# The last pair of a group of eight, its lent buffers, and the output transposes: another order for the same work

## The chip, the cores and the metric

The kernel runs on one core of one Trainium2 chip. The metric is the device time of one execution in microseconds. The kernel before took 1664.11 us as the median of 3 runs (1663.07 to 1665.39).

The engines are named as in the profile: PE is TensorE (matrix products and transposes), DVE is VectorE, ACT is ScalarE, POOL is GpSimd, SP is SyncE. Each works through its own instructions in the order in which the program writes them and waits, where it must, for what another engine has to deliver first.

## The reference

One layer of a diffusion backbone is applied to 640 tokens (128 context and 512 latent) of width 1024: a SwiGLU FFN as a half step, a token mixer (an mLSTM in both directions and a short convolution), a second SwiGLU FFN as a half step, and a final RMSNorm. The change lies in the second FFN and in the final norm:

```
h = modulate(rmsnorm(x, norm_g[2]), sh2, sc2)
a, b = split(h @ ffn2_w1, 2)              # 1024 -> 2 x 2816
x = x + 0.5 * g2 * ((silu(a) * b) @ ffn2_w2)   # 2816 -> 1024
y = rmsnorm(x, final_norm)                # all of it float32
```

## The kernel before

**Data.** Activations are kept transposed: a tile has 128 channels on its partitions and the 640 tokens along its free axis, in two halves of 320. The product of a 128 x 128 piece of a weight with 320 tokens is made from three matmuls (`three`, lines 242 to 247): the weight and the activation are each split into a rounded high part and a rest, and high x high, high x low and low x high are added up. A split (`split`, lines 73 to 79) is a cast on ACT (L75) and a subtraction on DVE (L79).

**Pairs.** `pair_el` takes two column blocks of a weight and both halves of the tokens as a 2 x 2 block product and does it with seven products instead of eight (`pair_steps`, from line 259). Their order is A11, S1, S2, A12, S3, S4, A22. Each takes 12 matmuls, and each uses one combination of the weights (S1 to S4 are sums or differences made on DVE, L218) and one combination of the activations: 11, 21, 22, T1, T2, T3, T4. Four PSUM tiles a, b, e, c gather the results: A11 goes into a; ACT copies a into b (L273), and S2 is added into b; ACT copies b into c (L283), and S3 is added into c; then c plus the result of S1 (called p5) is put into an SBUF tile (L294, or a copy on ACT and an addition on DVE, L291 and L292, where `spare_v` is set), after which A22 is added into c. The four results are given to the caller's function `ev(column block, half, source)`; the two of the second column block come last and are put into the list `late`.

**What sets the order.** There is no planner; the program order is written out by lists of functions. `flush` empties `late`; a pair does so in its first step, behind its product A11. The list `lazy` holds work that may come later (splits and differences of activations). `relax(n)` takes from it until fewer than n are left; after each of the seven steps a pair calls it with 9, 6, 5, 4, 3, 2 and 1. `fill` is a list that is spread over the steps of an element, and `at` gives functions for certain steps. Weights are cast and split four products ahead (`cast_more`), through a ring of five weight tiles named wr.

**The second FFN** (`ffn`, called at line 2120) takes the 22 hidden blocks in groups of 8, 8 and 6. The first two blocks run inside the element ahead of it (the head, `head_el`). A group of eight (`eights`) has a pair for each hidden block j: one column block is the half that goes through the silu, the other the half it is multiplied with (L1026 in `ev`). From the eight hidden blocks it then builds the seven combinations for the output product: `left` (high and low part of 11), `diff1` (T1, L1006) for j below 4; `diff2` (T2, L1010), `diff3` (21, L1015) and `diff4` (22, L1019) above. 11, T1, T2, 21 and 22 get buffers of their own; T3 and T4 are split into buffers that belong to the FFN's input and are lent (`put_lent`). They are lent once the last pair (j = 7) has read its own T3 and T4; their contents were stored to DRAM earlier in group 0 (`h_away`) and are loaded again afterwards (`h_back`). The tiles x, in which the differences are kept meanwhile, are borrowed too: POOL's queue writes x away and loads it again (`x_away`, `x_back`). Then four output pairs (m = 0, 2, 4, 6) multiply with the second weight and add into x (`add_x`, L945).

**The third group and the end.** Six hidden blocks are followed by eight output blocks: five in `plain_el` (both halves together, 36 matmuls each) and three in `halves_el` (all first halves, then all second halves). After each output block and half, `PO["y"]` appends a function `y_part(m, h)` to the list YQ: three transposes on PE into a PSUM tile of a ring of four (L2055), and three multiplications with the final norm's weights on DVE (L2061, L2067). When the last first half is there, `y_out` is appended: the mean squares of the first half's tokens (L826, L828), 12 scalings shared by ACT and DVE, and 12 output DMAs on SP. `halves_el` calls `y_after` at nine points; it empties YQ down to one entry, so at its first call ten parts in one go. The squares are added up on POOL (L808).

## Time and profile before

| | |
|---|---|
| median of 3 runs | 1664.11 us |
| the profiled execution, its own time | 1664.51 us |
| its span, first to last instruction | 1662.6 us |
| PE busy | 1633.0 us |
| DVE busy | 1317.9 us |
| ACT busy | 820.0 us |
| POOL busy | 221.7 us |
| mean granted clock of TensorE | 0.998 |

The span is what lies between the first and the last instruction; the time of the execution has 1.9 us around it. Busy times are those of the instructions alone. A row of the timeline gives start, duration, engine, line, operation, output and inputs, and in brackets for how long the engine stood idle before it and what ended that. A row of the waits gives who waited for whom: total, number of times, longest. A row of the windows gives the stretch and its length, then busy time and number of instructions of PE, PEld (weight loads), DVE, ACT and POOL, the granted clock, the DMA engines' busy share and GB/s.

### The profile page before, as it was taken

Reading aid. Unit: us, or ns where it says so; the run is one execution under the profiler, and the core shown is the slowest. Engines: PE = TensorE matmul, PEld = TensorE weight load, DVE = VectorE, ACT = ScalarE, POOL = GpSimd, SP = SyncE. Lnnn points to the kernel's source line nnn. Section 1 sums busy time; section 2 is a strip of 40 time slices with the busy share of each in tenths; the row PEclk is TensorE's granted clock in tenths of the full one; section 3 lists DMA queues with packets and bytes.
Section 4 is the critical chain, followed back from the end, with each engine's and each line's share of the span. In section 5 each row is a group of like instructions: output and inputs, shape, how many; then the busy total and the mean of one; then the engine's idle time right before and its main releaser. Section 6 shows DMA issues by size and latency. Waiting matters only on the chain.

```text
span 1662.6 us, 29463 instructions
## 1 busy us (share of the span) xinstructions
PE 1633.0 (98%) x11093; PEld 1587.7 (95%) x11093; DVE 1317.9 (79%) x2786; ACT 820.0 (49%) x1793; POOL 221.7 (13%) x354
## 2 busy tenths in 40 slices
PE   8999999999999999999999999999999999989997
PEld 5999999999999999999999999999999999989997
DVE  6867877877778878778887898789598887888765
ACT  5642542533566656555561455532375544554542
POOL 2010000000031322111122221011220011003001
PEclk9999999999999999999999999999999999999999
DMA  9454333343352434342367333367264265247421
GB/s 321 113 165 128 106 115 111 103 139 101 104 178 80 116 88 109 76 105 69 94 212 243 98 89 89 97 202 209 78 188 132 82 193 155 83 127 221 151 80 63
DMA packets 283661, 216.68 MB, mean 130 GB/s; under 512 B 9331, under 2 KB 260602, under 8 KB 283520
## 3 DMA queue, kind: packets, MB, share of 16 engines
q1 hardware_dynamic: 263152, 158.36, 33.2%
q0 software_dynamic: 20336, 56.45, 11.4%
q8 instruction: 87, 1.43, 0.4%
q14 instruction: 54, 0.44, 0.1%
q10 hardware_dynamic: 32, 0.01, 0.0%
HBM read 188.98 MB, written 25.79 MB: 129 GB/s over the span
## 4 chain that ended last, share of the span: by engine, by line
PE 84%; DVE 8%; ACT 4%; issue 2%; DMA 2%; SPq 0%; POOL 0%; POOLq 0%; ACTq 0%; DVEq 0%
PE ps L245 26%; PE ps L246 25%; PE ps L247 25%; DVE wl L79 2%; PE ax L1705 2%; PE ax L1736 2%; DVE ws L218 1%; PE ax L1708 1%; ACT wh L75 1%; DMA early<-in_w_mod_dram 1%; ACT Uh L859 1%; PE ax L1682 1%; DMA wr<-in_ffn_w_dram 0%; ACT Uh L75 0%; DVE x L945 0%
## 5 line engine op out<-in xcount | busy, mean ns | idle before, releaser
L79 DVE TENSOR_TENSOR wl<-wr,wh 128x512 fp32r<-128x512 f32 (+1 forms) x389 | 261.0, 683 | 78.2 <-ACT wh L75 76.1
L75 ACT CAST wh<-wr 128x512 fp32r<-128x512 f32 (+1 forms) x391 | 230.4, 600 | 89.2 <-PE ps L246 66.8
L75 ACT CAST wh<-ws 128x512 fp32r<-128x512 f32 x324 | 198.3, 619 | 122.8 <-DVE ws L218 77.8
L79 DVE TENSOR_TENSOR wl<-ws,wh 128x512 fp32r<-128x512 f32 x324 | 227.2, 701 | 39.1 <-ACT wh L75 38.4
L245 PE MATMUL ps<-Uh,wh 128*128 128x320 f32 x576 | 179.6, 312 | 4.7 <-ACT Uh L75 2.9
L246 PE MATMUL ps<-Ul,wh 128*128 128x320 f32 x576 | 177.9, 309 | 0.2
L247 PE MATMUL ps<-Uh,wl 128*128 128x320 f32 x576 | 177.7, 308 | 0.0
L245 PE MATMUL ps<-HT4h,wh 128*128 128x320 f32 x408 | 129.3, 317 | 4.9 <-DVE t L294 4.9
L246 PE MATMUL ps<-HT4l,wh 128*128 128x320 f32 x408 | 126.9, 311 | 0.1
L247 PE MATMUL ps<-HT4h,wl 128*128 128x320 f32 x408 | 126.7, 311 | 0.0
L245 PE MATMUL ps<-H11h,wh 128*128 128x320 f32 x376 | 118.8, 316 | 0.5 <-ACT H11h L75 0.5
L245 PE MATMUL ps<-H21h,wh 128*128 128x320 f32 x376 | 117.8, 313 | 0.0
L246 PE MATMUL ps<-H11l,wh 128*128 128x320 f32 x376 | 116.5, 310 | 0.3
L247 PE MATMUL ps<-H21h,wl 128*128 128x320 f32 x376 | 116.3, 309 | 0.0
L247 PE MATMUL ps<-H11h,wl 128*128 128x320 f32 x376 | 116.2, 309 | 0.0
L246 PE MATMUL ps<-H21l,wh 128*128 128x320 f32 x376 | 116.1, 309 | 0.0
L245 PEld LDWEIGHTS ps<-Uh,wh 128*128 128x128 f32 x576 | 108.3, 188 | 7.2 <-ACT Uh L75 3.8
L245 PE MATMUL ps<-HT3h,wh 128*128 128x320 f32 x356 | 111.8, 314 | 0.6 <-ACT ps L283 0.6
L945 DVE SCALAR_TENSOR_TENSOR x<-ps,modT,x 128x128 f32<-128x128 f32 (+2 forms) x176 | 66.0, 422 | 57.6 <-PE ps L247 57.0
L246 PE MATMUL ps<-HT3l,wh 128*128 128x320 f32 x356 | 110.0, 309 | 0.0
L247 PE MATMUL ps<-HT3h,wl 128*128 128x320 f32 x356 | 110.0, 309 | 0.0
L246 PEld LDWEIGHTS ps<-Ul,wh 128*128 128x128 f32 x576 | 108.3, 188 | 0.7 <-DVE Ul L79 0.7
(477 smaller groups left out, 4734.0 us busy)
## 6 DMA issues: line engine op xcount, KB each, us to landing
wr<-in_ffn_w_dram SPq DMA_DIRECT2D x102, 512.0 KB, 3.9
wr<-in_w_in_dram SPq DMA_DIRECT2D x72, 512.0 KB, 3.9
wr<-in_w_mod_dram SPq DMA_DIRECT2D x51, 512.0 KB, 3.9
wr<-in_ffn_w_dram SPq DMA_DIRECT2D x32, 384.0 KB, 3.3
xd<-x POOLq DMA_DIRECT2D x32, 320.0 KB, 5.8
x<-xd POOLq DMA_DIRECT2D x32, 320.0 KB, 4.0
early<-in_w_mod_dram SPq DMA_DIRECT2D x13, 512.0 KB, 8.8
mg<-in_w_mod_dram POOLq DMA_DIRECT2D x8, 512.0 KB, 5.6
```

The costliest lines, as they stand in the source:

```text
L75: A.copy(hi, raw)
L79: V.tensor_sub(lo, raw, f32(hi))
L218: getattr(engine, fn)(t, part(o, a), part(o, b))
L245: PE.matmul(ps, hi[:, ws], ah, start=start, stop=False, skip_group_check=True)
L246: PE.matmul(ps, hi[:, ws], al, start=False, stop=False, skip_group_check=True)
L247: PE.matmul(ps, lo[:, ws], ah, start=False, stop=stop, skip_group_check=True)
L859: A.activation(t[:, a:b], t[:, a:b], AF.Identity, scale=sc_, bias=bi_)
L945: V.scalar_tensor_tensor(x[:, o + a:o + b], ps[:, a:b], modT[:, g, m, cd:cd + 1], x[:, o + a:o + b], op0=OP.mult, op1=OP.add)
L1682: PE.matmul(p[:, :P], S["k", dt][:, sl], S["q", dt][:, sl], start=(dt == 0), stop=(dt == 1))
L1705: PE.matmul(p2[:, :DH + 1], S["q", dt][:, sl], S["C"][d][:, dt, :], start=(dt == 0), stop=(dt == 1))
L1708: PE.matmul(p1[:, :DH + 1], S["p", ch][:, d, :], PO["vt"][:, ch, :], start=True, stop=True)
L1736: PE.matmul(p[:, :DH + 1], kw[:, dt * P:(dt + 1) * P], PO["vt"][:, ch, :], start=True, stop=True)
```

## The change

1. **The last pair of a group (j = 7).** All three splits of T3 that can be made by then (`lent(0)` to `lent(2)`) are queued after product S3, and not one after each of S3, S4 and A22. After A22 the pair itself calls `flush` and `relax`: its two multiplications and its three differences with their splits are queued there, and not behind the first product of the output pair m = 0. In m = 0 the fourth T3 split moves from step 1 to step 0, and of the four T4 splits the third moves from step 2 to step 3.
2. **c + p5 by way of ACT.** `spare_v` is set for j = 7 and for all four output pairs of both groups of eight, and in group 0 for the first two pairs outside the head, j = 2 and j = 3 as well.
3. **A calm first pair.** In group 0 the first pair (j = 2) no longer calls `relax`: the head's leftover splits and differences stay in the list, and the next pair takes them up.
4. **The transposes.** Eight of the output parts are taken out of YQ by name and put into the fills of the output blocks 1 to 4 of the last group (1, 1, 3 and 3 of them). `y_after` takes at most two entries at a call, and `y_out` may go at the call after the first second half of `halves_el`, one call earlier.

```diff
-    def pair_el(load1, load2, ev, e1=None, spare_v=False, acts=HB, at=None):
+    def pair_el(load1, load2, ev, e1=None, spare_v=False, acts=HB, at=None, calm=False):
...
-                relax(7 - i if i else 9)
+                if not calm:
+                    relax(7 - i if i else 9)
...
+        spare = (n_head, n_head + 1, 7) if f0 < n_head else (7,)
...
-                at = {4: [relax, lent(0)], 5: [lent(1)], 6: [lent(2)]}
+                at = {4: [relax, lent(0), lent(1), lent(2)], 6: [flush, relax]}
...
-                grp.append(pair_el(*p, at={**at, **more.get(j, {})}))
+                grp.append(pair_el(*p, at={**at, **more.get(j, {})}, spare_v=j in spare, calm=f0 + j == n_head))
...
-                at = {0: [relax], 1: [lambda: put_lent("T3", 3, raw3(3))] + come(0, 1) + [four(0)],
-                      2: [four(1), four(2)], 3: [four(3)] + come(2, 3)}
+                at = {0: [lambda: put_lent("T3", 3, raw3(3))], 1: come(0, 1) + [four(0)],
+                      2: [four(1)], 3: [four(2), four(3)] + come(2, 3)}
...
-                               acts=UB, at=at))
+                               spare_v=True, acts=UB, at=at))
...
     def y_after(h, i):
-        while len(YQ) > 1:
-            YQ.pop(0)()
+        for _ in range(2):
+            if len(YQ) > 1 or h and i and YQ[:1] == [y_out]:
+                YQ.pop(0)()
...
         YQ.append(y_part(m, h))
+        YQ[-1].of = (m, h)
...
+    def y_next(m, h):
+        return step(lambda: YQ.pop(next(i for i, f in enumerate(YQ) if f.of == (m, h)))())
...
+    none = step(lambda: None)
+    for el, due in zip(els[2][1][1:-1], (((0, 0),), ((1, 0),), ((0, 1), (2, 0), (1, 1)), ((3, 0), (2, 1), (3, 1)))):
+        el["fill"] = [none] + [y_next(*q) for q in due] + [none]
```

## The prediction

> **What bounds the kernel now.** I read the page first, then who TensorE (PE) waited for from 1240 us on, where the second FFN begins (the functions that change serve only it), then the stretches around those waits.

> ```profile
> span 1662.6 us, 29463 instructions
> PE 1633.0 (98%) x11093; PEld 1587.7 (95%) x11093; DVE 1317.9 (79%) x2786; ACT 820.0 (49%) x1793; POOL 221.7 (13%) x354
> ```
> ```profile
> PE ps L245 <- DVE t L294: 4.9, 3, 1.8
> PE ps L245 <- ACT ps L273: 3.1, 3, 1.3
> PE ps L245 <- ACT Uh L75: 2.9, 2, 1.5
> PE ax L814 <- POOL sqacc L808: 0.3, 1, 0.3
> ```
> ```profile
> 1240.00:1260.00 20.00, 17.51 (x119) 17.00 (x118) 18.00 (x40) 11.46 (x27) 8.40 (x16) 1.00 0.68 184
> 1320.00:1334.30 14.30, 9.70 (x60) 8.42 (x58) 13.52 (x30) 8.90 (x21) 2.16 (x4) 1.00 0.51 146
> 1334.30:1337.80 3.50, 3.50 (x14) 3.50 (x15) 3.46 (x7) 0.71 (x2) 0.54 (x1) 0.51 0.43 164
> 1476.00:1489.50 13.50, 8.96 (x55) 7.69 (x53) 12.94 (x29) 8.18 (x20) 2.15 (x4) 1.00 0.53 155
> 1631.10:1636.70 5.60, 4.56 (x32) 3.12 (x31) 5.60 (x25) 0.47 (x1) 1.10 (x2) 1.00 0.00 0
> ```
> PE is the bound; what can be won is its idle time, and all of it that the change can reach lies in four places: the first pair of group 0 (1240 to 1260), the first output pair (m = 0) of each group of eight (1320, 1476), and the transposes in one heap (1631). In each, VectorE (DVE, third busy number) has next to no slack.

> Group 0 in PE rows. A product is 12 matmuls 0.147 us apart (1.76 us). The first number of a row is its start; the second is a latency, longer than the distance to the next start, so I work with starts.

> ```profile
> 1321.18 0.31 PE L247 MATMUL ps<-Uh,wl 128*128 128x320 f32 x1
> 1322.40 0.42 PE L245 MATMUL ps<-Uh,wh 128*128 128x320 f32 x1 [0.92 <-ACT ps L273]
> ...
> 1325.47 0.42 PE L245 MATMUL ps<-Uh,wh 128*128 128x320 f32 x1 [1.48 <-ACT Uh L75]
> ```
> ```profile
> 1334.21 0.51 PE L245 MATMUL ps<-HT4h,wh 128*128 128x320 f32 x1 [1.82 <-DVE t L294]
> ...
> 1337.45 0.47 PE L245 MATMUL ps<-Uh,wh 128*128 128x320 f32 x1
> ...
> 1489.48 0.42 PE L245 MATMUL ps<-HT4h,wh 128*128 128x320 f32 x1 [1.82 <-DVE t L294]
> ```
> Product S2 of m = 0 is due at 1321.33 and A22 four products (7.04) later, at 1328.4; A22 starts at 1334.21. So 5.8 us are lost, and then the clock is halved: A22 takes 1337.45 - 1334.21 = 3.24, 1.48 more than 1.76. Group 1 has the same waits (4.54 us of PE idle in its stretch of the table above, against 4.60) but a full clock.

> **The last pair (j = 7), both groups.** Its multiplications and differences no longer wait for m = 0's first product; but everything then stands in another order, so I lay the queues out again.

> ```profile
> 1314.43 0.48 DVE L294 TENSOR_TENSOR t<-ps,t 128x320 f32<-128x320 f32 x1
> 1314.83 0.48 DVE L1010 TENSOR_TENSOR x<-t,x 128x320 f32<-128x320 f32 x1
> 1315.83 0.49 DVE L79 TENSOR_TENSOR Ul<-x,Uh 128x320 fp32r<-128x320 f32 x1 [0.53 <-ACT Uh L75]
> ...
> 1318.25 0.68 DVE L79 TENSOR_TENSOR wl<-ws,wh 128x512 fp32r<-128x512 f32 x1
> 1318.86 0.48 DVE L297 TENSOR_TENSOR t<-ps,t 128x320 f32<-128x320 f32 x1
> ...
> 1323.52 0.48 DVE L1026 TENSOR_TENSOR t<-ps,t 128x320 f32<-128x320 f32 x1
> 1323.92 0.48 DVE L1026 TENSOR_TENSOR t<-t,t 128x320 f32<-128x320 f32 x1
> 1324.43 0.49 DVE L1010 TENSOR_TENSOR x<-t,x 128x320 f32<-128x320 f32 x1
> ```
> ```profile
> 1319.37 0.47 ACT L1024 ACTIVATE t<-t 128x320 f32<-128x320 f32 x1 [1.96 <-DVE t L297]
> 1320.10 0.61 ACT L75 CAST wh<-wr 128x512 fp32r<-128x512 f32 x1
> 1320.62 0.46 ACT L75 CAST HT3h<-x 128x320 fp32r<-128x320 f32 x1
> 1321.93 0.42 ACT L273 COPY ps<-ps 128x320 f32<-128x320 f32 x1
> 1324.96 0.46 ACT L75 CAST Uh<-x 128x320 fp32r<-128x320 f32 x1 [2.61 <-DVE x L1010]
> 1325.32 0.45 ACT L75 CAST Uh<-t 128x320 fp32r<-128x320 f32 x1
> ```
> Starts follow each other by 0.40 (DVE, 320 wide), 0.60 (DVE, 512), 0.36 (ACT, 320) and 0.52 (ACT, 512). On group 0's clock: ScalarE (ACT) copies c at 1314.43 (taken as L273's 0.42) and DVE adds p5 at 1314.90, 0.47 after today's L294. L1010 follows at 1315.30, its split at 1316.30. Then stand eight 320-wide instructions (two low halves, L1015, one low half, L1019, three T3 low halves; all three T3 splits are now here): to 1319.5. The wl of S2: 1320.1. L297: 1320.5. The sum for S3: 1321.1. The wl of A12 waits for the silu (1320.62) and its cast (1320.97 to 1321.59), so it runs 1321.62 to 1322.22; with half_gate, 1322.3. **Only there stand the multiplications**: L1026 at 1322.31 and 1322.71, L1010 at 1323.2: 1.2 earlier than today. The product they need (A22 of j = 7) ends two products before S2 is due, at 1317.8; it is DVE's queue that holds them, and queueing them earlier does not make it shorter.

> On ACT the change puts the three casts of those splits ahead of the cast for S3 and of the copy L273 (b from a), without which S2 cannot start: casts at 1323.76, 1324.12, 1324.48, S3's at 1324.84, L273 at 1325.36 to 1325.78. L273 stood at 1321.93; **it goes 3.4 us later**. S2 starts at 1325.84, a wait of 4.5 in one piece. After it nothing waits: T2 and T3 are split by then, c is copied off for S3 on time, and with c + p5 by way of ACT the copy follows S3's end by 0.1, so L294's 1.82 is gone. A22 starts at 1325.84 + 7.04 = 1332.9, not 1334.21: 1.3 won, 2.6 in both groups. Bounds of the wait: 1.1 (L273 as today) to 5.5 (another 1.0 on DVE).

> **The clock.** The table above gives 0.51 of the clock over 3.5 us, so about 3.4 us at one half, right after a wait of 1.82 (2.0 by starts). Group 1's equal wait had no such consequence. I read this as a judgement over stretches of that length, which a wait of 2.0 trips if it falls into one stretch and misses if it falls across two. A wait of 4.5 leaves more than 2 in one of them wherever it falls, so I charge the 1.48 in both groups: 3.0 in place of 1.5, a loss of 1.5. Bounds: 0.4 a group (the half stretch falls mostly into the wait itself) to 2.3 (a second stretch is tripped).
> [...]

> The other output pairs and j = 7 get one ACT copy of 0.42 each: ACT is at 49%, and no PE wait lies in those pairs. POOL's reloads of x keep their place behind the T3 and T4 splits and go earlier with them; the first output that needs one is added after product A12. Price nothing; if the cover went, 0.42 a pair.

> **The first pairs of group 0.**

> ```profile
> 1252.71 0.38 PE L245 MATMUL ps<-HT4h,wh 128*128 128x320 f32 x1 [1.24 <-DVE t L294]
> 1259.47 0.41 PE L245 MATMUL ps<-HT2h,wh 128*128 128x320 f32 x1 [1.25 <-ACT ps L273]
> ```
> ```profile
> 1250.14 0.62 ACT L75 CAST wh<-ws 128x512 fp32r<-128x512 f32 x1 [1.55 <-DVE ws L218]
> ```
> These idle times are counted from a latency's end; by starts they are 1.40 each, 2.8. The first goes: ACT's copy of c stands behind the cast at 1250.14, so at 1250.7, and is done by 1251.1, before A22 is due at 1252.71 - 1.40 = 1251.3. The second (L273 behind the cast of a difference) goes with the six leftovers of the head that j = 2 no longer runs. But these run in j = 3, together with j = 2's own two. DVE's load in a pair is seven low halves and four sums of 0.60, two additions for c and p5 and two multiplications of 0.40, in all 8.2; to that come in j = 3 three low halves and three differences with theirs (9 of 0.40) and put_ (0.3), 12.1 in the pair's 12.3 us, and j = 2 ends some 2 us behind. So the backlog stays: the last difference comes at 1268.4, its cast at 1268.9, L273 of j = 4 behind it and the cast for S3 at 1269.8 to 1270.2, while S2 of j = 4 is due at 1268.9: 1.25 late. Won: 2.8 - 1.25 = **1.55**; bounds 0 and 2.8. The silu tiles that the leftovers hold longer are read before their ring of eight comes round to them in j = 3 and 4; price nothing.

> **The transposes.**

> ```profile
> 1631.17 1.47 PE L2055 MATMUL ax<-ident,x 128*128 128x128 f32 x12
> 1633.45 3.51 PE L2055 MATMUL ax<-ident,x 128*128 128x128 f32 x18 [0.81 <-DVE H11h L2067]
> 1636.72 0.39 PE L245 MATMUL ps<-Uh,wh 128*128 128x320 f32 x1
> ...
> 1639.45 0.49 PE L2055 MATMUL ax<-ident,x 128*128 128x128 f32 x3
> 1639.70 0.39 PE L245 MATMUL ps<-Uh,wh 128*128 128x320 f32 x1
> 1639.93 0.31 PE L246 MATMUL ps<-Ul,wh 128*128 128x320 f32 x1
> ```
> The heap of ten parts takes PE from 1631.17 to 1636.72 plus 0.08 (the matmul after it takes 0.23): 5.63, because four buffers wait for DVE's 30 multiplications. A part alone costs 0.25 + 0.08 = 0.33. Eight parts go into outputs 1 to 4 (2.64), two stay together, six transposes at 0.11 plus 0.08 (0.73). Won 5.63 - 3.37 = **2.26**; bounds 0 (each part waits 0.3 for DVE) and 2.6. At most three parts fall on one output of 5.3 us, with four buffers, so none waits. y_out, with its 12 output DMAs on SP, goes half an output earlier, which takes its scalings from ahead of the last squares: POOL's 0.3 before L814 goes.

> **Sum.** The profiled execution took 1664.51 (span 1662.6 and 1.9 around it), 0.4 over the median 1664.11. 1664.51 - 2.6 + 1.5 - 1.55 - 2.26 - 0.3 = 1659.3; against the median 1658.9. I say **1659.2**.

> **Rivals.**
> 1. The wait at S2 half as long or gone, as it would be if DVE's queue were short at j = 7. With it gone: 1664.5 - 11.6 (5.8 twice) - 1.5 - 1.55 - 2.56 = 1647.3; half as long (2.25 twice, no half clock) 1651.8. Against it: L1026 ran 5.6 us after its product. Chance 0.12.
> 2. [...] Chance 0.08.
> 3. No change: the head's waits only move to j = 3 and j = 4 (1.55 lost) and the half clock costs 2.3 in both groups (1.6 lost): 1662.4. For it: DVE is busy 18.0 of 20 us in 1240 to 1260. Chance 0.15.
> 4. Slower: the T3 splits. Two of them now stand 2.4 and 3.0 us earlier than any row shows T3's buffers free (cast of 1320.62). If they wait until then, all behind them on ACT and DVE, L273 last, is 3.0 later, and the longer wait trips a second half-clock stretch (0.8 more): 3.8 in both groups, 1666.9. It makes the kernel slower from 2.4 a group on, and measurably so from 4.1. Against it: the first T3 split ran without a wait, and the matmuls that read T3 end where L294 could start, at 1314.4. Chance 0.10.

> My forecast has 0.55, by itself 1657.3 to 1661.3. A measurement of this kernel tells about 0.2%, 3.3 us: faster means below 1660.8, slower above 1667.4. Faster holds the forecast but for a tenth of it, and rivals 1 and 2: 0.70. No change takes that tenth, rival 3 and half of rival 4: 0.25. Slower has the other half: 0.05. The range, 1653 to 1662.5, leaves out rival 4 and most of rival 1.

> **What would show it.** In the first output pair of each group one PE wait before S2, named ACT L273, of about 4.5, and no wait for DVE L294; L273 behind three casts; half clock after it in both. A wait of some 1.2 for L273 in j = 4. Transposes in threes among outputs 1 to 4, no heap. I am wrong if the S2 wait is under 3 or split up, if a clock stays full after it, or if PE stands before a transpose.

## The result, and the profile after

The changed kernel took **1659.1 us** as the median of 9 runs (1657.47 to 1660.07), the kernel before 1663.6 us in 9 runs beside it. The ratio is 0.9972, with an interval of 0.9962 to 0.9983: 0.28% faster. The execution profiled took 1660.07 us, 4.4 less than the 1664.51 of the one before.

The page of the changed kernel, its head:

```profile
span 1658.2 us, 29450 instructions
PE 1631.9 (98%) x11093; PEld 1589.7 (96%) x11093; DVE 1320.3 (80%) x2786; ACT 825.0 (50%) x1805; POOL 221.9 (13%) x354
```

PE's work is unchanged, ACT has its 12 more copies. The waits of PE from 1236 to 1652 us (total, times, longest):

```profile
PE ps L245 <- ACT ps L273: 7.4, 3, 3.2
PE ps L245 <- DVE t L297: 2.0, 2, 1.0
```

The kernel before has six rows here, the four of the prediction, 0.8 us for L2067 ahead of a transpose and 0.6 for L283; they are two now. The waits for L294, for the cast L75, for L283, for L2067 and for POOL's L808 (now L809) are gone. What is left is L273, longer than before, and **a new name, L297**. Stretch by stretch, first the kernel before (stretch and length; busy time of PE, PEld, DVE, ACT, POOL; clock; DMA share; GB/s):

```profile
1317.70:1337.40 19.70, 15.10 (x86) 13.75 (x85) 18.22 (x39) 10.24 (x23) 2.71 (x5) 0.92 0.43 127
1473.00:1491.30 18.30, 13.76 (x86) 12.35 (x85) 16.82 (x36) 9.63 (x22) 2.15 (x4) 1.00 0.44 129
```

and the kernel after:

```profile
1240.00:1260.00 20.00, 20.00 (x140) 20.00 (x139) 18.99 (x41) 13.45 (x30) 8.44 (x16) 1.00 0.77 211
1260.00:1272.00 12.00, 10.87 (x74) 10.62 (x73) 10.03 (x21) 6.88 (x16) 0.00 (x0) 1.00 0.16 48
1316.10:1335.80 19.70, 15.54 (x86) 15.02 (x85) 17.59 (x38) 10.32 (x24) 2.25 (x5) 0.83 0.42 121
1319.97:1323.38 3.41, 1.14 (x8) 0.87 (x6) 2.76 (x7) 1.25 (x5) 0.00 (x0) 1.00 0.12 51
1323.40:1330.20 6.80, 5.94 (x22) 5.94 (x23) 6.11 (x13) 5.36 (x13) 1.09 (x2) 0.50 0.49 129
1471.20:1489.70 18.50, 14.41 (x86) 13.88 (x85) 17.46 (x37) 10.22 (x24) 2.25 (x5) 0.91 0.44 129
1480.40:1483.80 3.40, 3.40 (x15) 3.40 (x14) 3.40 (x7) 3.37 (x9) 0.56 (x2) 0.50 0.68 171
1600.00:1640.00 40.00, 39.88 (x281) 39.38 (x280) 26.61 (x76) 12.88 (x31) 6.90 (x8) 1.00 0.09 25
```

The first stretch is the first pair outside the head: full where it had 17.51. The stretches of 19.70 and 18.50 reach from the start of the first output pair's A11 to that of the next pair's A11. **They are as long as before** (19.70 and 18.30): PE's idle time in them is shorter, and the clock is lower. The last row is where the heap of transposes was: PE now stands for 0.12 us of 40.

Where the 4.4 us came from can be read off the starts of the same instructions. A11 of j = 2 starts at 1240.44, where it was 1240.30; A11 of the first output pair of group 0 at 1316.14, where it was 1317.72: **1.72** from the head. The next pair's A11 is 1.61 earlier (1335.84 for 1337.45), in group 1 the two are 1.78 and 1.63 earlier: the first output pairs gave **nothing** (0.03 won, then 0.15 lost). From the third group's output blocks (1.63 earlier) to the end the lead grows to 4.43: **2.80** from the end part.

PE's rows in the changed kernel, j = 4 of group 0, then both first output pairs:

```profile
1270.32 0.41 PE L245 MATMUL ps<-HT2h,wh 128*128 128x320 f32 x1 [1.13 <-ACT ps L273]
...
1317.75 0.31 PE L247 MATMUL ps<-Uh,wl 128*128 128x320 f32 x1
1319.07 0.42 PE L245 MATMUL ps<-Uh,wh 128*128 128x320 f32 x1 [1.01 <-DVE t L297]
...
1320.80 0.31 PE L247 MATMUL ps<-Uh,wl 128*128 128x320 f32 x1
1324.26 0.63 PE L245 MATMUL ps<-Uh,wh 128*128 128x320 f32 x1 [3.15 <-ACT ps L273]
...
1474.16 0.42 PE L245 MATMUL ps<-Uh,wh 128*128 128x320 f32 x1 [1.01 <-DVE t L297]
...
1479.28 0.41 PE L245 MATMUL ps<-Uh,wh 128*128 128x320 f32 x1 [3.08 <-ACT ps L273]
```

By starts (a matmul is 0.147 long) the two waits of group 0 are 1319.07 - 1317.75 - 0.147 = 1.17 and 1324.26 - 1320.80 - 0.147 = 3.31: 4.48 in all, the first before product S1, the second before S2. What DVE and then ACT were doing meanwhile:

```profile
1317.93 0.68 DVE L79 TENSOR_TENSOR wl<-ws,wh 128x512 fp32r<-128x512 f32 x1
1318.53 0.48 DVE L297 TENSOR_TENSOR t<-ps,t 128x320 f32<-128x320 f32 x1
...
1320.75 0.48 DVE L1028 TENSOR_TENSOR t<-ps,t 128x320 f32<-128x320 f32 x1
...
1321.66 0.49 DVE L1012 TENSOR_TENSOR x<-t,x 128x320 f32<-128x320 f32 x1
```
```profile
1322.19 0.46 ACT L75 CAST Uh<-x 128x320 fp32r<-128x320 f32 x1 [2.16 <-DVE x L1012]
...
1322.91 0.45 ACT L75 CAST x<-t 128x320 fp32r<-128x320 f32 x1
1323.27 0.61 ACT L75 CAST wh<-ws 128x512 fp32r<-128x512 f32 x1
1323.79 0.41 ACT L273 COPY ps<-ps 128x320 f32<-128x320 f32 x1
```

This is the queue of the prediction: the multiplications (now L1028) stand behind the sums and splits of weights, the casts of the differences behind them, and L273 last.

### The profile page after: what moved, and what is told of

The parts are those of the page before. It is cut to its first block, busy times and chain, and to the rows that moved or that the text cites. A ratio compares the mean times of both kernels' runs of the same rounds, so it can differ in the third digit from the quotient of the medians.

```text
span 1658.2 us, 29450 instructions
## 1 busy us (share of the span) xinstructions
PE 1631.9 (98%) x11093; PEld 1589.7 (96%) x11093; DVE 1320.3 (80%) x2786; ACT 825.0 (50%) x1805; POOL 221.9 (13%) x354
## 4 chain that ended last, share of the span: by engine, by line
PE 89%; DVE 5%; ACT 3%; DMA 2%; SPq 1%; issue 1%; POOL 0%; ACTq 0%; DVEq 0%; POOLq 0%
PE ps L245 27%; PE ps L246 27%; PE ps L247 27%; PE ax L1707 2%; PE ax L1738 2%; DVE wl L79 1%; DMA wr<-in_ffn_w_dram 1%; PE ax L1710 1%; ACT wh L75 1%; PE ax L1684 1%; ACT Uh L860 1%; DMA wh<-in_x_sample_dram 0%; DVE ws L218 0%; DVE Uh L852 0%; PE ax L709 0%
## 5 line engine op out<-in xcount | busy, mean ns | idle before, releaser
L79 DVE TENSOR_TENSOR wl<-wr,wh 128x512 fp32r<-128x512 f32 (+1 forms) x389 | 261.2, 683 | 79.2 <-ACT wh L75 76.0
L75 ACT CAST wh<-wr 128x512 fp32r<-128x512 f32 (+1 forms) x391 | 230.4, 600 | 89.2 <-PE ps L246 70.8
L79 DVE TENSOR_TENSOR wl<-ws,wh 128x512 fp32r<-128x512 f32 x324 | 228.3, 705 | 37.2 <-ACT wh L75 36.3
L75 ACT CAST wh<-ws 128x512 fp32r<-128x512 f32 x324 | 198.4, 619 | 104.6 <-DVE ws L218 64.7
L245 PE MATMUL ps<-Uh,wh 128*128 128x320 f32 x576 | 182.0, 316 | 8.3 <-ACT ps L273 6.2
L246 PE MATMUL ps<-Ul,wh 128*128 128x320 f32 x576 | 179.5, 312 | 0.0
L247 PE MATMUL ps<-Uh,wl 128*128 128x320 f32 x576 | 179.4, 312 | 0.0
L245 PE MATMUL ps<-HT4h,wh 128*128 128x320 f32 x408 | 128.4, 315 | 0.0
L246 PE MATMUL ps<-HT4l,wh 128*128 128x320 f32 x408 | 126.2, 309 | 0.1
L247 PE MATMUL ps<-HT4h,wl 128*128 128x320 f32 x408 | 126.1, 309 | 0.0
L245 PEld LDWEIGHTS ps<-Uh,wh 128*128 128x128 f32 x576 | 109.7, 191 | 10.5 <-ACT ps L273 6.8
L245 PE MATMUL ps<-H11h,wh 128*128 128x320 f32 x376 | 118.8, 316 | 0.5 <-ACT H11h L75 0.5
L245 PE MATMUL ps<-H21h,wh 128*128 128x320 f32 x376 | 117.7, 313 | 0.0
L246 PE MATMUL ps<-H11l,wh 128*128 128x320 f32 x376 | 116.5, 310 | 0.3
L247 PE MATMUL ps<-H21h,wl 128*128 128x320 f32 x376 | 116.2, 309 | 0.0
L247 PE MATMUL ps<-H11h,wl 128*128 128x320 f32 x376 | 116.2, 309 | 0.0
L246 PE MATMUL ps<-H21l,wh 128*128 128x320 f32 x376 | 116.0, 308 | 0.0
L245 PE MATMUL ps<-HT3h,wh 128*128 128x320 f32 x356 | 111.6, 313 | 0.0
L246 PE MATMUL ps<-HT3l,wh 128*128 128x320 f32 x356 | 110.0, 309 | 0.0
L247 PE MATMUL ps<-HT3h,wl 128*128 128x320 f32 x356 | 110.0, 309 | 0.0
L246 PEld LDWEIGHTS ps<-Ul,wh 128*128 128x128 f32 x576 | 109.8, 191 | 0.0
L247 PEld LDWEIGHTS ps<-Uh,wl 128*128 128x128 f32 x576 | 109.7, 190 | 0.0
```

Source lines behind the costliest of these rows:

```text
L75: A.copy(hi, raw)
L79: V.tensor_sub(lo, raw, f32(hi))
L245: PE.matmul(ps, hi[:, ws], ah, start=start, stop=False, skip_group_check=True)
L246: PE.matmul(ps, hi[:, ws], al, start=False, stop=False, skip_group_check=True)
L247: PE.matmul(ps, lo[:, ws], ah, start=False, stop=stop, skip_group_check=True)
```

## The experiments

Theory: the change is three parts that do not touch each other. The head gives some 1.6 us, the end part some 2.8, and the last pair's new order gives nothing, because the time that it takes out of PE's waits comes back as half clock. The rivals: the last pair's gain was never there, whatever the clock does (the waits move and no more); or the copies L291 (part 2 of the change) do the work and the new order spoils it.

**One part at a time.** `y_only` has part 4 (the transposes) alone, `y_after` and the names of the parts included.

```diff
...
+    for el, due in zip(els[2][1][1:-1], (((0, 0),), ((1, 0),), ((0, 1), (2, 0), (1, 1)), ((3, 0), (2, 1), (3, 1)))):
+        el["fill"] = [none] + [y_next(*q) for q in due] + [none]
```

> The transposes alone, on the kernel before. Theory (the parts add up; the heap cost PE 5.6 us and spread parts cost 0.33 each): 2.8 us faster than the kernel before, as the two traces differ from the start of the third group's outputs on. Rival (the heap's time was covered by the additions for the second halves, or the gain needs the earlier parts of the change): under 1 us.

Measured: 1660.91 us against 1663.52 of before on the same chip, ratio 0.9983 [0.9974, 0.9992]: 2.6 us. The windows of its trace, the end part:

```profile
1600.00:1640.00 40.00, 39.88 (x281) 39.38 (x280) 26.59 (x75) 12.89 (x31) 6.91 (x8) 1.00 0.09 26
```

The same 39.88 of 40 as with the whole change: the end part's gain is its own.

`head_only` has part 3 (calm) and the copies of part 2 in j = 2 and j = 3 of group 0.

```diff
+                if not calm:
+                    relax(7 - i if i else 9)
...
+        spare = (n_head, n_head + 1) if f0 < n_head else ()
...
-                grp.append(pair_el(*p, at={**at, **more.get(j, {})}))
+                grp.append(pair_el(*p, at={**at, **more.get(j, {})}, spare_v=j in spare, calm=f0 + j == n_head))
```

> Only the calm first pair and c + p5 by ScalarE in j = 2 and j = 3. Theory: the two waits of 1.4 us go and one of about 1.3 us comes in j = 4, before product S2: 1.6 us faster. Rival (the leftovers only move, and each comes back as a wait): 0.

Measured: 1662.61 us, 0.9992 [0.9983, 1.0001]: 0.9, with an interval that takes in both nothing and the 1.6 looked for. Its trace is clearer than its times. The waits of PE from 1236 to 1300 us:

```profile
PE ps L245 <- ACT ps L273: 1.1, 1, 1.1
```

PE's rows for A11 of j = 2, then S2 and A22 of the first output pair of group 0, and a window in that pair, which this kernel doesn't change:

```profile
1241.52 0.31 PE L245 MATMUL ps<-H11h,wh 128*128 128x320 f32 x1
...
1322.00 0.42 PE L245 MATMUL ps<-Uh,wh 128*128 128x320 f32 x1 [0.93 <-ACT ps L273]
...
1333.82 0.41 PE L245 MATMUL ps<-HT4h,wh 128*128 128x320 f32 x1 [1.10 <-DVE t L294]
```
```profile
1325.00:1328.40 3.40, 3.33 (x11) 3.09 (x12) 3.35 (x8) 3.40 (x10) 0.00 (x0) 0.51 0.23 67
```

and of the kernel before, its A11 of j = 2:

```profile
1240.30 0.31 PE L245 MATMUL ps<-H11h,wh 128*128 128x320 f32 x1
```

From A11 of j = 2 to S2 it takes 80.48 us, before 1322.40 - 1240.30 = 82.10: the head gives 1.62, with one wait in j = 4 left, as in the whole change. But this execution is 1.22 late when j = 2 begins, in code that no kernel here changes, and such differences between executions are what blurs a median. Something else is to be seen: the half clock, which before fell on A22, falls on the last quarter of S2 and on A12 here (1325.04 to 1328.45), and costs nothing there. From S2 to A22 it is 11.82 us, before 1334.21 - 1322.40 = 11.81, because A22 waits for L294 in any case, only 1.10 instead of 1.82. (In `y_only`, which leaves this pair as it was, half clock begins at 1326.21, in the kernel before at 1334.37.)

`last_only` has part 1 and part 2 for j = 7 and the output pairs.

```diff
-                at = {4: [relax, lent(0)], 5: [lent(1)], 6: [lent(2)]}
+                at = {4: [relax, lent(0), lent(1), lent(2)], 6: [flush, relax]}
...
+                grp.append(pair_el(*p, at={**at, **more.get(j, {})}, spare_v=j == 7))
...
-                at = {0: [relax], 1: [lambda: put_lent("T3", 3, raw3(3))] + come(0, 1) + [four(0)],
-                      2: [four(1), four(2)], 3: [four(3)] + come(2, 3)}
+                at = {0: [lambda: put_lent("T3", 3, raw3(3))], 1: come(0, 1) + [four(0)],
+                      2: [four(1)], 3: [four(2), four(3)] + come(2, 3)}
...
+                               spare_v=True, acts=UB, at=at))
```

> Only the last pair's new order with the lent splits, and c + p5 by ScalarE in j = 7 and in the output pairs. Theory (DVE's queue sets the multiplications, and the wait in one piece of 4.5 us trips the half clock in both groups): between 1 us faster and 0.5 us slower; half clock in both groups in the profile, 3.4 to 6.8 us each. Rival (the waits saved are kept): 2.6 us faster or more.

Measured: 1663.38 us, 0.9998 [0.9990, 1.0007]: nothing. The windows from A11 of the first output pair to A11 of the next:

```profile
1318.00:1336.60 18.60, 14.43 (x87) 13.91 (x86) 17.42 (x38) 10.30 (x23) 2.18 (x5) 0.91 0.43 128
1472.00:1490.50 18.50, 14.41 (x86) 13.89 (x86) 17.08 (x37) 10.26 (x23) 2.17 (x4) 0.91 0.44 128
```

Here group 0 takes 18.6 with one half-clock stretch, in the changed kernel 19.7 with two. The waits are the same to 0.02 us. So the three parts add up (2.6 + 0.9 + 0.1 = 3.6 of 4.5 by the medians, the rest within the intervals), and the half clock differs by a whole stretch from one profiled execution to the other.

**The copies without the new order.** `spare_only` sets `spare_v` for j = 7 and the output pairs and leaves every `at` as before.

```diff
+                grp.append(pair_el(*p, at={**at, **more.get(j, {})}, spare_v=j == 7))
...
+                               spare_v=True, acts=UB, at=at))
```

> Only c + p5 by ScalarE in j = 7 and in the output pairs; multiplications and lent splits stand as before. Theory: the wait of 2.0 us before A22 goes; 0.35 us before S1 comes (the addition of p5 stands later on DVE); the others stay in pieces of at most 1.7 us, too scattered to trip the half clock: some 1.5 us a group and the half clock's share, 3 to 4.5 us faster in all, so more than the whole of the last pair's change. Rival (it is the queueing at once that wins): under 1.5 us.

Measured: 1661.87 us, 0.9987 [0.9978, 0.9996]: 1.65 us. The windows of its trace: group 0 from A11 to A11, then its half-clock stretch and the stretch ahead of that; and the first of PE's waits from 1310 to 1345 us:

```profile
1317.40:1334.70 17.30, 14.63 (x86) 13.61 (x85) 15.86 (x35) 10.08 (x24) 2.16 (x4) 0.90 0.42 122
1325.30:1328.70 3.40, 3.10 (x11) 2.86 (x12) 3.12 (x8) 3.40 (x10) 0.00 (x0) 0.50 0.28 84
1321.90:1325.30 3.40, 1.59 (x9) 1.32 (x9) 3.12 (x8) 0.79 (x3) 0.00 (x0) 1.00 0.57 166
```
```profile
PE ps L245 <- ACT Uh L75: 1.5, 1, 1.5
```

The copy does what it is meant to: A22 of the first output pair no longer waits for L294, and the pair takes 17.3 instead of 19.7. The expectation of a full clock was **wrong**. I had held these waits (1.5 us the longest) for too scattered to lower the clock, but in the stretch ahead of the half clock they add up to 3.40 - 1.59 = 1.8 us of idle PE, and half clock followed, in group 1 too (1.5 us of idle PE there; its row is in the last section). Here the half clock is paid: L294's wait, which hid it in `head_only`, is gone.

**The whole change with the old order.** `after_old_order` is the changed kernel with the two old `at` lists.

```diff
-                at = {4: [relax, lent(0), lent(1), lent(2)], 6: [flush, relax]}
+                at = {4: [relax, lent(0)], 5: [lent(1)], 6: [lent(2)]}
...
-                at = {0: [lambda: put_lent("T3", 3, raw3(3))], 1: come(0, 1) + [four(0)],
-                      2: [four(1)], 3: [four(2), four(3)] + come(2, 3)}
+                at = {0: [relax], 1: [lambda: put_lent("T3", 3, raw3(3))] + come(0, 1) + [four(0)],
+                      2: [four(1), four(2)], 3: [four(3)] + come(2, 3)}
```

> The changed kernel with the last pair's multiplications, differences and lent splits where they stood before; all else of the change stays. Theory (the new order gathers the waits of m = 0 into fewer, longer ones and wins nothing on the queue): as c + p5 by ScalarE alone won 1.65 us and with the new order nothing, it is 1 to 2 us faster than the changed kernel, about 1657.5 us. Rival (with the head's waits gone the new order pays): slower than the changed kernel, 1660 us or more.

Measured: 1656.98 us against 1663.46, 0.9955 [0.9943, 0.9968]; the changed kernel has 1659.1 and 0.9972. **The new order costs about 2 us.** The two kernels were not run beside each other, and their intervals overlap a little; by the ratios it is 2.8 us. `last_only` against `spare_only`, the same difference on one chip, gives 1.5. The windows of the two first output pairs:

```profile
1316.30:1333.60 17.30, 14.64 (x85) 13.61 (x85) 15.86 (x35) 10.04 (x24) 2.17 (x4) 0.90 0.43 124
1469.00:1486.60 17.60, 14.89 (x86) 13.88 (x85) 16.16 (x35) 10.18 (x24) 2.17 (x4) 0.90 0.44 128
```

17.3 and 17.6 with one half-clock stretch each, against 19.7 and 18.5. The copies are the part of the last pair's change that gains.

**The clock by itself.** `after_busy` is the changed kernel with matrix products that nobody reads, 7 ahead of S1 and 22 ahead of S2 of each first output pair. They fill the two waits, read what is there already and write a spare PSUM tile.

```diff
+            pre, mid = busy.get(name, (0, 0))
+            spin = aux() if pre or mid else None
             for kk in range(4):
+                for _ in range(pre if kk == 0 else mid if kk == 3 else 0):
+                    PE.matmul(spin[:, :HT], hi[:, :P], acts[ACT_OF[name]][0][0], start=True, stop=True, ...)
...
-                               spare_v=True, acts=UB, at=at))
+                               spare_v=True, acts=UB, at=at, busy={"S1": (7, 0), "S2": (22, 0)} if m == 0 else {}))
```

> The changed kernel with idle products put in: 7 matmuls ahead of S1 and 22 ahead of S2 in the first output pair of both groups, into a PSUM tile that nobody reads, so that TensorE is not idle in the 1.2 and 3.3 us for which it waits there. The result is not touched. Theory (the half clock after these waits costs 1.5 to 3 us a group): the profile shows no half clock in either group, and the kernel is 3 to 4 us faster than the changed one, about 1655.5 us. Rival (the products after the wait would not run faster at full clock, being bound by DVE and ACT, or the granted clock has another cause): 1659 us or more, as the added matmuls can only delay.

Measured: 1656.23 us against 1663.46, 0.9957 [0.9944, 0.9969], 2.9 under the changed kernel (2.5 by the ratios; the two were not run beside each other). PE's rows of the added products in group 0, and the windows of the two first output pairs:

```profile
1318.13 1.19 PE L269 MATMUL ax<-Uh,wh 128*128 128x320 f32 x7
...
1321.16 3.39 PE L269 MATMUL ax<-Uh,wh 128*128 128x320 f32 x22
```
```profile
1316.40:1333.40 17.00, 17.00 (x114) 16.56 (x114) 15.99 (x35) 10.18 (x23) 2.17 (x4) 1.00 0.43 127
1468.80:1485.70 16.90, 16.90 (x115) 16.54 (x114) 15.89 (x34) 10.21 (x23) 2.16 (x4) 1.00 0.44 126
```

This settles the main question. The waits are as long as before: from A11 to the first matmul of S2 it is 8.12 us in group 0 and 8.04 in group 1, in both kernels. PE is only kept busy in them; the clock stays at 1.00, and the pairs take 17.0 and 16.9 instead of 19.7 and 18.5. The half clock costs 2.7 in group 0 and 1.6 in group 1 of the profiled executions, and 2.9 of the median. The waits themselves are still there: the pairs would take 12.3 us without them.

**A better order.** `mix` keeps parts 2, 3 and 4. In j = 7 it queues two T3 splits, and the multiplications after A22 as the change does, but not the differences behind them; these come with the first product of m = 0 again, and the other two T3 splits in its step 1.

```diff
-                at = {4: [relax, lent(0), lent(1), lent(2)], 6: [flush, relax]}
+                at = {4: [relax, lent(0), lent(1)], 6: [flush]}
...
-                at = {0: [lambda: put_lent("T3", 3, raw3(3))], 1: come(0, 1) + [four(0)],
-                      2: [four(1)], 3: [four(2), four(3)] + come(2, 3)}
+                lent3 = lambda k: lambda: put_lent("T3", k, raw3(k))
+                at = {0: [relax], 1: come(0) + [lent3(2), lent3(3)] + come(1), 2: [four(0), four(1)],
+                      3: [four(2), four(3)] + come(2, 3)}
```

> The changed kernel with another order of the last pair: two T3 splits after S3 in j = 7 (not three), the multiplications still queued at its end, but the differences and their splits only behind the first product of m = 0 and its copy, so that the copy of a into b does not stand behind them; the other T3 splits in step 1, T4's in steps 2 and 3. Theory (DVE's queue in this order is 0.8 us a group shorter and the wait falls into pieces of 0.8, 1.9 and 0.5 us): 1.5 to 3 us faster than the changed kernel, 1656 to 1657.5 us, half clock in some executions. Rival (DVE's total is the bound, the order does not matter): 1659 us.

Measured: 1654.31 us against 1663.46, 0.9943 [0.9930, 0.9955], better than expected. The windows of the first output pairs and the two longest of PE's waits from 1236 to 1600 us:

```profile
1316.60:1332.40 15.80, 13.52 (x86) 12.41 (x85) 14.83 (x33) 9.23 (x23) 2.17 (x4) 1.00 0.42 111
1468.30:1484.00 15.70, 13.50 (x87) 12.40 (x86) 14.73 (x32) 9.21 (x22) 2.17 (x4) 1.00 0.42 123
```
```profile
PE ps L245 <- ACT Uh L75: 2.5, 2, 1.3
PE ps L245 <- ACT ps L273: 1.5, 3, 1.1
```

L273 no longer stands behind the casts of the differences, no wait is longer than 1.3, and the clock stays full. The expected pieces of 0.8, 1.9 and 0.5 us came as 0.77, 1.82 and 0.45 in group 0, by starts; better than expected is the clock, 0.998 or 0.999 in all five executions against 0.995 to 0.997 in those of the changed kernel. So both go down here, the waits (15.8 us against 17.0 in `after_busy`) and the half clock.

`mix_busy` fills those waits with idle products (4 ahead of S1, 12 inside S2, 2 ahead of S3).

```diff
+                               spare_v=True, acts=UB, at=at, busy={"S1": (4, 0), "S2": (0, 12), "S3": (2, 0)} if m == 0 else {}))
```

> The same order with idle products in its waits: 4 ahead of S1, 12 ahead of the last quarter of S2, 2 ahead of S3 in the first output pair of both groups. Theory: no half clock, and both savings together: 1654 us, the fastest. Rival (as for the two before): 1657 us or more.

Measured: 1654.55 us, 0.9944 [0.9930, 0.9958]: no difference from `mix`. Where the clock was full already, idle products won nothing; the gain of `after_busy` was the clock's and not an effect of the products as such.

**What calm does.** `mix_no_calm` is `mix` without part 3; `mix_slack` has a softer form of it, in which j = 2, 3 and 4 keep 2, 2 and 1 more entries in `lazy`.

```diff
-                grp.append(pair_el(*p, at={**at, **more.get(j, {})}, spare_v=j in spare, calm=f0 + j == n_head))
+                grp.append(pair_el(*p, at={**at, **more.get(j, {})}, spare_v=j in spare))
```

> The mixed order, but the first pair of group 0 calls relax as every pair does, so the head's leftovers run in j = 2 again; c + p5 stays by ScalarE in j = 2 and j = 3. It asks which half of the head's change wins. Theory (ScalarE's copy removes only the wait before A22; the copy of a into b in j = 3 stands behind a difference's cast all the same, and further behind, as PE arrives earlier): a wait of 2.5 to 3 us before S2 of j = 3 in place of the 1.3 us in j = 4, so 1.5 us slower than the mixed order, 1655.8 us. Rival (c + p5 by ScalarE is what wins, the calm pair only moves work): no slower than the mixed order, 1654.3 us.

```diff
-                if not calm:
-                    relax(7 - i if i else 9)
+                relax(7 - i + slack if i else 9)
...
-                grp.append(pair_el(*p, at={**at, **more.get(j, {})}, spare_v=j in spare, calm=f0 + j == n_head))
+                grp.append(pair_el(*p, at={**at, **more.get(j, {})}, spare_v=j in spare, slack={n_head: 2, n_head + 1: 2, n_head + 2: 1}.get(f0 + j, 0)))
```

> The mixed order, with the head's leftovers spread instead of held back: relax leaves 2 more entries than usual in j = 2 and j = 3 and 1 more in j = 4. It asks whether the wait of 1.3 us in j = 4 comes from eight leftovers in one pair. Theory (it does; DVE has room in j = 5 and j = 6): the wait before S2 of j = 4 goes, one of at most 0.3 us comes later, 0.8 us faster than the mixed order, 1653.5 us. Rival (the backlog is not the leftovers' but the pairs' own): the wait stays, 1654.3 us.

Measured, against 1664.55 of before: 1655.93 us, 0.9954 [0.9939, 0.9969], without calm, and **1653.78 us, 0.9939 [0.9922, 0.9955]**, with slack, the fastest kernel of the study, 10.8 us under the kernel before and 2.2 under `mix_no_calm` on the same chip. The longest of PE's waits of `mix_no_calm` from 1236 to 1320 us, then the windows of `mix_slack`:

```profile
PE ps L245 <- ACT ps L273: 2.3, 1, 2.3
```
```profile
1240.00:1260.00 20.00, 19.94 (x137) 19.68 (x136) 19.29 (x43) 13.34 (x30) 8.41 (x16) 1.00 0.76 208
1260.00:1272.00 12.00, 12.00 (x84) 12.00 (x83) 9.76 (x19) 6.62 (x16) 0.00 (x0) 1.00 0.28 81
```

Without calm the backlog hits j = 3 as one wait of 2.3 for L273; with calm 1.1 of it moves to j = 4 and the rest is absorbed; with slack spread over three pairs the two stretches of 20 and 12 us are full but for 0.06. Its lead over `mix` (0.5 us), and the 1.6 us between `mix` and `mix_no_calm`, were not measured on one chip.

## Why the prediction was right, and where it was not

The predicted 1659.2 and the measured 1659.1 agree better than the terms do. Against the profiled execution, step by step:

| step | predicted | measured |
|---|---|---|
| head | -1.55 | -1.72 |
| waits of the first output pairs | -2.6 | -2.5 |
| half clock | +1.5 | +2.6 |
| transposes and POOL | -2.56 | -2.80 |
| elsewhere | 0 | 0.0 |
| sum | -5.2 | -4.4 |

The waits are what is left of the distance from A11 to A11 after seven products (12.32 us) and the half clock: 5.93 and 6.02 before (19.73 and 18.34 in full figures), 4.74 and 4.69 after (19.70 and 18.49). "Elsewhere" is 0.14 lost ahead of j = 2 and 0.17 won between the two groups' output pairs; 0.16 of that is half clock of before that reached over into the next pair's A11, where two matmuls took 0.45 us and now take 0.29. The profiled execution went 0.8 less far than the sum; the median of the nine runs lies 1.0 below that execution. The two make up for each other, and that is luck.

**The head** came as worked out, wait for wait: two of 1.40 gone, one of 1.28 by starts in j = 4 for L273, predicted 1.25. These make 1.52; the other 0.2 lies in gaps of 0.1 us and less. The working by queue held: the last of the three differences was to run at 1268.4 and its cast at 1268.9, and they ran at 1268.44 and 1268.96 (in an execution that is 0.14 later there). `mix_slack` shows that this rest was not forced by DVE's load: spread further, it is hidden.

**The waits of the last pair.** The sum was right (4.48 for 4.5) and the picture wrong: "a wait of 4.5 in one piece", and "I am wrong if the S2 wait is under 3 or split up". It is split, 1.17 ahead of S1 for L297 and 3.31 ahead of S2 for L273. The queue itself was laid out well. With the 1.58 us added by which all is earlier in the changed kernel, L297 starts at 1320.11 (it was to run from 1320.1 to 1320.5), the multiplications at 1322.33 (1322.31), L273 at 1325.37 (1325.36) and S2 at 1325.84 (1325.84). The step that failed is the one behind it: that only S2 waits for this queue. The prediction moved L297 from 1318.86 to 1320.1 and never asked who waits for it. S1 starts a new PSUM tile (e), which takes the buffer of the pair ahead's b, and L297 is what reads b last; the wait of S1 is put down to L297 in both groups. S1 was due at 1319.48 on the time axis of before. With L297 at 1318.86 it was covered, if barely; at 1320.11 it was not. L273, and with it the end of the wait for S2, stands in ACT's queue behind the same casts either way, so the sum stays the same.

**The clock.** It was right that the longer wait brings half clock in both groups, and the changes of the clock do lie 3.41 us or a multiple of it apart (the last section has the figures); the size was too small. Predicted were 3.0 us for both; in the profiled execution it is 2.6 in group 0 (22 matmuls, 0.267 instead of 0.147 us apart) and 1.5 in group 1, 4.1 in all. The second stretch in group 0, which I had only as a bound, is real, and its 2.6 is more than the 2.3 of that bound. `after_busy` puts the whole price at 2.9 us of the median. The last pair's net gain, forecast at 1.1, is nothing (`last_only`: 0.1).

**The transposes** were as predicted in kind, with the size 0.24 under. PE among outputs 1 to 4, in the place of the heap, and behind it:

```profile
1619.65 0.49 PE L2057 MATMUL ax<-ident,x 128*128 128x128 f32 x3
...
1632.19 0.82 PE L2057 MATMUL ax<-ident,x 128*128 128x128 f32 x6
...
1638.46 1.37 PE L2057 MATMUL ax<-ident,x 128*128 128x128 f32 x6
```

None of the first two stands behind a wait, and none for POOL comes after. In the last row two of six transposes start 0.39 and 0.33 us after the one ahead, where 0.11 is usual: 0.5 us in all, by the trace's releasers for DVE's L946. So PE does stand before a transpose, though hardly. `y_only` gives the end part alone: 2.6.

**The rivals.** Rival 4 (T3's buffers not free) falls: the three casts of T3 run on ACT in one go from 1315.30 and their low halves on DVE from 1316.72, each right behind the instruction ahead; L273 is 3.4 later through the casts of the differences, as forecast. Rival 1 (the wait at S2 gone) falls with the 3.15. Behind the 0.08 of rival 2, which is part of the 0.70 for faster, stands nothing that a run shows: the stretch ahead of the half clock was not idle throughout, PE was busy for 1.14 of 3.41 us of it in the changed kernel and for 1.59 of 3.40 in `spare_only`. Rival 3 had one half right: the last pair brought nothing, through the half clock, as it said (2.6 and 1.5 us where it had 2.3 twice). Its other half, that the head's waits only move, fell.

What the prediction did not ask is which of its parts gains. It read parts 1 and 2 as one, and credited both with L294's wait. `spare_only` and `after_old_order` show that the copy on ACT alone takes away that wait, and that the order laid out beside it, with the casts of the differences ahead of L273, costs some 2 us.

## What to carry to other kernels

When work is queued earlier on a busy engine, list for every instruction that goes later who reads its result and which buffer it frees; here S1 waited for the last reader of the PSUM tile whose buffer it took, and no name in the code says so. Price a wait of PE together with the clock that follows it, and before tuning the wait away, fill it with products that nobody reads: what that wins is the clock's part of the price (2.9 us here), and what is left is the wait's. Of a change in several parts run each alone; here one part gave nothing and hid a better order, worth 5 us more.

## What the runs showed of the hardware

Nor did it need one long wait. Of the stretches of 3.41 us on that grid (windows, in what follows), the one right ahead of half clock has PE busy for 1.59 us in the kernel before, and the two in the changed kernel for 1.14 and 1.12; every other window between the first and the last products has 1.91 or more in the kernel before and 2.03 or more in the changed kernel. The rows nearest to each other in other executions, a window of `spare_only` (half clock followed) and one of `mix_no_calm` (it did not):

```profile
1475.49:1478.90 3.41, 1.90 (x11) 1.41 (x11) 2.85 (x7) 1.15 (x4) 0.00 (x0) 1.00 0.70 224
1258.17:1261.58 3.41, 1.83 (x12) 1.83 (x13) 2.88 (x7) 2.77 (x6) 0.00 (x0) 1.00 0.06 17
```

So 1.51 us of idle PE in a window was followed by half clock, and 1.58 was not; the two rows overlap, and no limit can be read from busy times. In group 0 of `spare_only` the 1.8 us of idle PE ahead of half clock came from two waits, of 0.97 and 1.48. In group 0 of `mix`, no 3.41 us of the first output pair has PE busy for less than 2.03, wherever one lays the window, and the clock stayed full. In the kernel before, group 1 had the waits of group 0 and a full clock: they fell otherwise on the grid, and its windows have 1.91 or more, against 1.59 ahead of the half clock in group 0. Nor did half clock always cost: in `head_only` it fell where the next product had to wait anyway (11.82 us from S2 to A22, and 11.81 in the kernel before).

Executions differ before the changed code begins: A11 of j = 2 starts at 1240.09 to 1241.52 in the ten profiled kernels whose rows show it, which are alike up to there, and the grid begins at 10.00 in one trace and at 9.25 in the other. So where the waits fall in the windows differs as well. Two things stay open: whether a limit lies near those 1.5 us, and why in group 0 of the changed kernel a second half stretch followed the first. PE stood for 0.87 us of that first one, at most 0.30 us of any other whose rows were read (`spare_only`, group 0); that the wait which reached over into it kept the clock down was not tried by itself.
